# A two-block fp32 network on one core: reciprocal roots of the memory norm and of two head norms on GpSimd, and a new order of work at the ends of the MLPs and of the last head

## The chip, the cores and the metric

One Trainium2 chip, of which the program uses one core. The metric is the device time of one execution in microseconds; the time before is the median of three runs. Engines are named as the profile does: PE is TensorE, DVE is VectorE, ACT is ScalarE, POOL is GpSimd, SP is SyncE, which issues most loads.

## The reference

All in fp32, 512 tokens of width 1024, 256 memory rows, 4 delta-rule heads of 128. Cut to what matters here:

```python
def rmsnorm(x, g):
    return x * rsqrt(mean(x * x, -1) + EPS) * g

def first_block(x, mem, ...):
    h = rmsnorm(x, norm_mix)
    x = x + hybrid_mixer(h, ...)          # chunk gating and a gated delta rule, 4 heads
    m = rmsnorm(mem, norm_mem)            # the memory's norm
    x = x + memory_cross_attention(rmsnorm(x, norm_xa), m, ...)   # keys m @ w_k, values m @ w_v
    x = x + square(relu(rmsnorm(x, norm_ffn) @ w1)) @ w2          # first MLP, width 4096
    return rmsnorm(x, norm_final)

# in hybrid_mixer, for each head:
    o = rmsnorm(gated_delta_rule(q, k, v, g, beta), dn_onorm) * silu(gate)   # the head's output norm
    ... concatenate([y_a, o]) @ w_out

def second_block(x, p, ...):              # mLSTM, sliding-window attention, merge, then
    x = x + square(relu(rmsnorm(x, norm_mlp) @ w_up)) @ w_down    # second MLP
    gate = sigmoid(rmsnorm(x, norm_ple) @ w_ple_gate)
    x = x + gate * (p @ w_ple_proj)       # p is 512 x 256
    return rmsnorm(x, final_norm)
```

## The kernel before

Activations stay in SBUF with features on the partitions, 128 to a tile and 512 tokens wide. A product in fp32 is made of three matmuls on rounded parts (`mm3`, L282 to L284): high by high, high by low and low by high. So every weight granule (`wload`) is loaded by SP into a raw buffer `wr`, rounded by ACT into `wh` (L263) and subtracted by DVE into `wl` (L264); an activation is split in the same way by `split_sb`, ACT L324 or L327 for the high part, DVE L325 or L328 for the remainder. Products of the projections go into three psum banks `psd`; small products of the heads go into banks `c`, two of each kind.

Each engine runs its instructions in the order in which the scheduler put them when the program was built. The scheduler takes what is ready by priority, which is the order of the code unless `high_priority(n)` moves a piece n steps ahead; `issue_after(x)` puts an instruction behind x, and `hold(n)` puts a piece behind the n-th `mm3` that follows.

Norms. `tok_rs` sums the squares `acc` over the partitions with a matmul by ones (L345), DVE adds epsilon (L347), and `rsqrt` takes the reciprocal root: with `power` one POOL instruction (L181), without it eleven small DVE instructions (L186, L187, and three rounds of L189 to L191). `tok_bc` copies the result out wide (DVE L354), transposes it on PE (L357) and copies the psum (ACT L359); that is the scale `bc` with which the psum of the next projection is taken out.

The delta rule. Its four heads run in generators interleaved with the projections. A head inverts a triangular matrix on DVE in 15 steps of two small instructions (L681, L683), with small DMA transfers on SP ahead and behind (L678, L685) and small matmuls after (L661). At its end it takes the norm of its output (L757 to L768: factor `dsc`, scaled output `do`), and `fin` transposes the output (PE L773) and splits it (L327, L328) into `yb`. While heads 2 and 3 run, the memory's norm and its key and value projections (`memory`) are done; keys leave psum by DVE L812. Then `w_out1` multiplies the four heads' `yb` by `w_out_b`, four granules of two output tiles, and adds the result to `x`.

The MLPs. The second product runs by a Strassen-Winograd form, `st_gemm`: per granule, seven products of 12 matmuls of 256 columns into psum banks X, Z (`x` in the rows) and Y (`psd`), each followed by an addition into `x_fm` on DVE (L982) before its bank is used again. `st_weights` loads and splits the parts (L324, L325; the sum of two parts is L959). POOL issues DMA transfers that accumulate sums of weight blocks in memory for it (L229, `sums_ffn_w`), each after copies that ACT's queue issues (L225) have landed. In the last quarter, `post` does the next norm's work for each finished tile: split (L327, L328) and squares (ACT L337, DVE L338). `between` does this for the first MLP, with two sums of squares, and `tail` for the second; `tail` then multiplies `p`, which it splits with L324 and L325, by `w_ple_proj`.

## Time and profile before

| | |
|---|---|
| median of 3 runs | 1700.75 us (1698.43 to 1703.73) |
| the profiled execution | 1699.93 us, of which the span is 1698.1 us |
| PE busy | 1677.7 us, 99% |
| PE weight loads | 1455.5 us, 86% (beside the matmuls) |
| DVE busy | 1207.7 us, 71% |
| ACT busy | 821.5 us, 48% |
| POOL busy | 72.2 us, 4% |
| granted TensorE clock | 1.000 over the span |

The span is what the profiler saw of the program; 1.8 us of the execution lie around it. Busy shares are means over stages. An idle time of PE stands in its timeline in square brackets, with what ended it.

### The profile page before, as it was taken

How to read it: one execution, taken by the hardware profiler on the slowest of the kernel's cores; microseconds unless marked ns; L12 is line 12 of the kernel's file. 1: busy time of each engine (PE TensorE's matmuls, PEld its weight loads, DVE VectorE, ACT ScalarE, POOL GpSimd, SP SyncE). 2: the span in 40 equal slices, each digit the busy share in tenths (PEclk: the TensorE clock that was granted, in tenths of full speed). 3: DMA queues.
4: the chain of work that ended last, by engine and by line, in shares of the span. 5: the costliest groups of instructions: out<-in, count | busy, mean ns of one | idle time of the engine just before them, and what ended most of it. 6: DMA issues, size and time to landing. Idle time of an engine off the chain costs nothing.

```text
span 1698.1 us, 25916 instructions
## 1 busy us (share of the span) xinstructions
PE 1677.7 (99%) x9916; PEld 1455.5 (86%) x9916; DVE 1207.7 (71%) x2521; ACT 821.5 (48%) x1462; POOL 72.2 (4%) x92
## 2 busy tenths in 40 slices
PE   9999999999999999999999999999999999999998
PEld 8988898887898989889988887788888989898987
DVE  6988886656686868688845569865566767676865
ACT  5355755444444444454444457654234444444554
POOL 0200001000000000000000000000000000000000
PEclk9999999999999999999999999999999999999999
DMA  6321366545546464423333332334464464644331
GB/s 203 101 76 52 96 154 180 135 99 174 121 130 170 127 170 128 132 92 110 103 90 97 100 88 69 94 88 115 118 189 126 130 172 124 172 125 133 100 112 50
DMA packets 81947, 205.63 MB, mean 121 GB/s; under 512 B 13088, under 2 KB 14240, under 8 KB 81824
## 3 DMA queue, kind: packets, MB, share of 16 engines
q1 hardware_dynamic: 62672, 169.29, 31.9%
q0 software_dynamic: 9216, 16.78, 7.1%
q10 hardware_dynamic: 9936, 17.91, 3.8%
q8 instruction: 78, 1.28, 0.3%
q14 instruction: 45, 0.37, 0.1%
HBM read 201.59 MB, written 35.65 MB: 140 GB/s over the span
## 4 chain that ended last, share of the span: by engine, by line
PE 88%; DVE 7%; ACT 2%; issue 1%; DMA 1%; SPq 0%; ACTq 0%; DVEq 0%
PE psd L283 21%; PE psd L284 21%; PE psd L282 21%; PE x L282 5%; PE x L283 5%; PE x L284 5%; DVE wl L264 1%; PE c L661 1%; PE c L607 1%; PE lg L1344 1%; PE po L1371 1%; ACT wh L263 1%; DVE S L437 1%; PE m L1265 1%; DVE acc L338 1%
## 5 line engine op out<-in xcount | busy, mean ns | idle before, releaser
L284 PE MATMUL psd<-S,wl 128*128 128x512 f32 (+1 forms) x1256 | 484.1, 386 | 2.6 <-DVE wl L264 2.5
L282 PE MATMUL psd<-S,wh 128*128 128x512 f32 (+1 forms) x1256 | 483.1, 385 | 0.7 <-ACT S L327 0.7
L283 PE MATMUL psd<-S,wh 128*128 128x512 f32 (+1 forms) x1192 | 458.6, 385 | 1.1 <-DVE S L328 0.8
L284 PEld LDWEIGHTS psd<-S,wl 128*128 128x128 f32 x1256 | 236.3, 188 | 48.1 <-DVE wl L264 3.7
L282 PEld LDWEIGHTS psd<-S,wh 128*128 128x128 f32 x1256 | 236.5, 188 | 45.6 <-ACT S L327 1.1
L264 DVE TENSOR_TENSOR wl<-wr,wh 128x1024 fp32r<-128x1024 f32 (+2 forms) x160 | 192.2, 1201 | 116.3 <-ACT wh L263 115.6
L283 PEld LDWEIGHTS psd<-S,wh 128*128 128x128 f32 x1192 | 224.2, 188 | 44.3 <-DVE S L325 1.5
L263 ACT CAST wh<-wr 128x1024 fp32r<-128x1024 f32 (+2 forms) x160 | 163.9, 1026 | 154.7 <-PE psd L283 107.2
L284 PE MATMUL psd<-wh,S 128*128 128x256 f32 (+2 forms) x480 | 135.8, 283 | 0.0
L282 PE MATMUL psd<-wh,S 128*128 128x256 f32 (+2 forms) x480 | 135.7, 283 | 0.0
L283 PE MATMUL psd<-wl,S 128*128 128x256 f32 (+2 forms) x480 | 135.2, 282 | 0.0
L282 PE MATMUL x<-S,wh 128*128 128x256 f32 x452 | 128.0, 285 | 2.9 <-DVE x_fm L982 2.8
L283 PE MATMUL x<-S,wh 128*128 128x256 f32 x452 | 126.5, 281 | 0.0
L284 PE MATMUL x<-S,wl 128*128 128x256 f32 x452 | 126.0, 280 | 0.0
L283 PE MATMUL psd<-S,whx 128*128 128x512 f32 (+1 forms) x296 | 107.8, 364 | 1.0 <-DVE S L325 0.9
L282 PE MATMUL psd<-S,whx 128*128 128x512 f32 (+1 forms) x296 | 107.8, 365 | 0.0
L284 PE MATMUL psd<-S,wlx 128*128 128x512 f32 (+1 forms) x296 | 107.5, 363 | 0.0
L982 DVE TENSOR_TENSOR x_fm<-x_fm,x 128x256 f32<-128x256 f32 x192 | 78.5, 415 | 27.4 <-PE x L284 27.1
L282 PEld LDWEIGHTS psd<-wh,S 128*128 128x128 f32 x480 | 90.4, 189 | 0.3
L283 PEld LDWEIGHTS psd<-wl,S 128*128 128x128 f32 x480 | 90.3, 188 | 0.3
L284 PEld LDWEIGHTS psd<-wh,S 128*128 128x128 f32 x480 | 90.4, 188 | 0.1
L282 PEld LDWEIGHTS x<-S,wh 128*128 128x128 f32 x452 | 84.8, 188 | 5.8 <-DVE x_fm L982 3.1
(455 smaller groups left out, 3176.3 us busy)
## 6 DMA issues: line engine op xcount, KB each, us to landing
wrx<-in_ffn_w_dram SPq DMA_DIRECT2D x32, 512.0 KB
wrx<-in_w_up_dram SPq DMA_DIRECT2D x20, 512.0 KB
wr<-in_w_in_qk_dram SPq DMA_DIRECT2D x16, 512.0 KB
sums_ffn_w<-in_ffn_w_dram ACTq DMA_DIRECT2D x32, 256.0 KB
wr<-in_ffn_w_dram SPq DMA_DIRECT2D x16, 512.0 KB
sums_w_down<-in_w_down_dram ACTq DMA_DIRECT2D x32, 256.0 KB
wr<-in_w_in_v_dram SPq DMA_DIRECT2D x12, 512.0 KB
wr<-in_w_up_dram SPq DMA_DIRECT2D x12, 512.0 KB
```

What stands on the lines that cost most here:

```text
L263: self.last_cast = nc.scalar.copy(hi[:, c], raw[:, c])
L264: nc.vector.tensor_tensor(out=lo[:, c], in0=raw[:, c], in1=hi[:, c].bitcast(F32), op=ALU.subtract)
L282: mm(ps, ah, bh, start=first, stop=False, skip_group_check=more)
L283: mm(ps, ah, bl, start=False, stop=False, skip_group_check=more)
L284: self.last_mm = mm(ps, al, bh, start=False, stop=last, skip_group_check=more)
L338: nc.vector.tensor_tensor(out=acc, in0=acc, in1=sq, op=ALU.add)
L437: nc.vector.tensor_scalar(out=d, in0=d, scalar1=ag[:, j, 0:1], scalar2=r[:, j:j + 1], op0=ALU.subtract, op1=ALU.mult)
L607: nc.tensor.matmul(blk(ps, b), lhs(b), rhs(b), start=True, stop=True)
L661: nc.tensor.matmul(ps[:, b * n:(b + 1) * n], lhs[:, b], rhs(b), start=True, stop=True)
L982: TT(out=x[n][t], in0=x[n][t], in1=ps, op=op)
L1265: nc.tensor.matmul(pX[:, :W], PT[:, tt], va[:, tt], start=True, stop=True)
L1344: nc.tensor.matmul(ps[:, i, K0:], qs[:, 2 * e2 + i, cs], kd[:, w, kc], start=(w == 0), stop=(w == 1))
```

## The change

Six edits, in the order of the program.

1. The output norms of heads 0 and 1 and the norm of the memory take their reciprocal root by the power on POOL in place of the eleven DVE instructions. The memory's `tok_bc` is held behind the 15th `mm3`.
2. In `w_out1` the first granule is written out: k = 0, 1, 2 of both output tiles, then k = 3 (head 3) of both. The cast of the second granule is put behind the cast of head 3's `yb`.
3. In `st_weights` and `st_gemm` the splits, the sum L959 and the additions L982 get a priority 400 steps ahead.
4. The split of a norm's input in `between` and in `tail` gets 200 steps ahead; the squares stay where they were.
5. In `between` the column sums are held behind the 8th `mm3`, and the transposes of the two scales behind the 21st in place of the 16th.
6. In `tail` the split of `p` and the copies of its product get 400 steps ahead.

```diff
 def wload(self, src, kt, n, pieces=None, behind=None):
...
+            with self.tc.issue_after(behind.ins) if behind else nullcontext():
+                self.last_cast = nc.scalar.copy(hi[:, c], raw[:, c])
...
-    def norm_tile(self, k, xh, xl, acc, gname):
-        self.split_sb(xh[k], xl[k], self.x[:, k], self.vcol(gname, k))
+    def norm_tile(self, k, xh, xl, acc, gname, ahead=0):
+        with self.tc.high_priority(ahead):
+            self.split_sb(xh[k], xl[k], self.x[:, k], self.vcol(gname, k))
         self.sq_acc(acc, self.x[:, k], k)
...
-        f = self.rsqrt(mp, so, 4, "do")
+        f = self.rsqrt(mp, so, 4, "do", h < 2)
...
-        for g in range(4):
-            self.proj_fm(self.wgran("w_out_b", g, nk=4), *self.yb, (2 * g, 2 * g + 1), ev)
+        wh, wl = self.wgran("w_out_b", 0, nk=4)
+        (yh, yl), ps = self.yb, [self.psd() for _ in range(2)]
+        for ks in ((0, 1, 2), (3,)):
+            for j in range(2):
+                for k in ks:
+                    c = slice(j * P, (j + 1) * P)
+                    self.mm3(ps[j], wh[k][:, c], wl[k][:, c], yh[k], yl[k], k == 0, k == 3)
+        for j in range(2):
+            ev(j, ps[j])
+        for g in range(1, 4):
+            w = self.wgran("w_out_b", g, nk=4, behind=self.yb_cast if g == 1 else None)
+            self.proj_fm(w, *self.yb, (2 * g, 2 * g + 1), ev)
...
-        rs = self.tok_rs(acc, "rsm", 2)
-        bc = self.tok_bc(rs, "bcm", 2)
+        rs = self.tok_rs(acc, "rsm", 2, power=True)
+        with self.hold(15):
+            bc = self.tok_bc(rs, "bcm", 2)
...
         def split(raw, hi, lo, c=slice(0, 2)):
-            self.split_sb(hi[:, c], lo[:, c], raw[:, c])
+            with self.tc.high_priority(400):
+                self.split_sb(hi[:, c], lo[:, c], raw[:, c])
...
-        nc.vector.tensor_tensor(out=A[0], in0=A[0], in1=B[0], op=ALU.add)
+        with self.tc.high_priority(400):
+            nc.vector.tensor_tensor(out=A[0], in0=A[0], in1=B[0], op=ALU.add)
...
         def add(n, t, ps, op=ALU.add):
-            TT(out=x[n][t], in0=x[n][t], in1=ps, op=op)
+            with self.tc.high_priority(400):
+                TT(out=x[n][t], in0=x[n][t], in1=ps, op=op)
...
-            self.split_sb(xh[o], xl[o], self.x[:, o], g12[:, o:o + 1])
+            with self.tc.high_priority(200):
+                self.split_sb(xh[o], xl[o], self.x[:, o], g12[:, o:o + 1])
...
-            r1 = self.tok_rs(acc, "rs", power=True)
-            ps = self.pss()
+            with self.hold(8):
+                r1 = self.tok_rs(acc, "rs", power=True)
+                ps = self.pss()
...
-            with self.hold(16):
+            with self.hold(21):
...
-            self.norm_tile(o, *ops, "norm_ple_g_2")
+            self.norm_tile(o, *ops, "norm_ple_g_2", 200)
...
-                self.split_sb(ph[:, i], ph[:, 2 + i], raw[:, i])
+                with self.tc.high_priority(400):
+                    self.split_sb(ph[:, i], ph[:, 2 + i], raw[:, i])
```

The rows below are the instructions of one engine in the order in which it runs them. Rows of the changed kernel carry its own line numbers, a few higher than those of before (L265 is L264 of before, L349 is L347, L356 is L354, L329 is L328, L340 is L338, L1000 is L982).

The first place is the memory's norm. On POOL, before, after the last of the products of the first gating stage, the accumulating transfers follow one another:

```order
L442 TENSOR_TENSOR S_42_358<-S_42_358,S_41_357 128x256
L229 DMA sums_ffn_w_0_63<-in_ffn_w_dram 128x512
L229 DMA sums_ffn_w_0_63<-sums_ffn_w_0_63 128x512
L229 DMA sums_ffn_w_1_64<-in_ffn_w_dram 128x512
L229 DMA sums_ffn_w_1_64<-sums_ffn_w_1_64 128x512
```

The same piece after, with `doy` the factor of a head's norm and `rsmy` that of the memory's:

```order
L445 TENSOR_TENSOR S_42_358<-S_42_358,S_41_357 128x256
L181 TENSOR_TENSOR doy_1500<-dso_1489,mhalf 128x4
L229 DMA sums_ffn_w_0_63<-in_ffn_w_dram 128x512
L181 TENSOR_TENSOR doy_1859<-dso_1848,mhalf 128x4
L229 DMA sums_ffn_w_0_63<-sums_ffn_w_0_63 128x512
L181 TENSOR_TENSOR rsmy_2700<-rsmv_2698,mhalf 128x2
L229 DMA sums_ffn_w_1_64<-in_ffn_w_dram 128x512
```

Each of the three powers stands ahead of one of the first three accumulating transfers, and behind the one before it.

On DVE, before, this is a piece of the memory norm's Newton steps (`rsm`), among head 2's inversion; `wl_2756` is the second half of the first key granule:

```order
L189 TENSOR_TENSOR rsmt_2726<-rsmy_2725 128x2
L264 TENSOR_TENSOR wl_2756<-wr_2754,wh_2755 128x1024
L683 TENSOR_TENSOR dV_2283<-dV_2283,dA_402_2284 32x2x14
L190 SCALAR_TENSOR_TENSOR rsmt_2726<-rsmt_2726,rsmv_2722 128x2
L665 TENSOR_TENSOR dT_2825<-dM_2576,masks 128x512
L681 TENSOR_TENSOR dA_402_2284<-dV_2283 32x15
L191 SCALAR_TENSOR_TENSOR rsmy_2725<-rsmt_2726,rsmy_2725 128x2
L675 MEMSET dV_2835 32x256
L683 TENSOR_TENSOR dV_2283<-dV_2283,dA_402_2284 32x15
L189 TENSOR_TENSOR rsmt_2726<-rsmy_2725 128x2
L676 MEMSET dV_2835 32x16
L665 TENSOR_TENSOR dA_402_2284<-dM_2255,masks 128x512
```

And after, from the subtraction for the second key granule's first half over L349 (the sum that the power takes) to the copy L356 (the power's result):

```order
L684 TENSOR_TENSOR dA_398_2260<-dV_2259 32x7x9
L190 SCALAR_TENSOR_TENSOR drt_2503<-drt_2503,dss_2481 128x8
L265 TENSOR_TENSOR wl_2990<-wr_2988,wh_2989 128x1024
L686 TENSOR_TENSOR dV_2259<-dV_2259,dA_398_2260 32x7x9
L191 SCALAR_TENSOR_TENSOR dry_2502<-drt_2503,dry_2502 128x8
L349 TENSOR_SCALAR rsmv_2698<-pss_2695 128x2
L684 TENSOR_TENSOR dA_398_2260<-dV_2259 32x6x10
L189 TENSOR_TENSOR drt_2503<-dry_2502 128x8
L356 COPY e_494_2702<-rsmy_2700 128x256
L686 TENSOR_TENSOR dV_2259<-dV_2259,dA_398_2260 32x6x10
L190 SCALAR_TENSOR_TENSOR drt_2503<-drt_2503,dss_2481 128x8
```

Before, L354 followed six rows further on, fifty behind L347; now the copy stands three rows behind the sum, in the middle of head 2's inversion, and the subtraction for the first key granule's second half has moved far ahead of both.

The second place is the end of the last head, on ACT. Before, `do` is head 3's output, `c_619` its transpose, and `wh_3582` the second granule of `w_out_b`:

```order
L327 ACTIVATE S_592_3237<-psd_3471,rsmy_2725 128x256
L768 ACTIVATE do_2949<-do_2949,dsc_2998 128x128 x4
L263 CAST wh_3582<-wr_3581 128x1024
L327 ACTIVATE S_176_1231<-c_619_3450,vec 128x512
L327 ACTIVATE S_592_3237<-psd_3498,rsmy_2725 128x256
L225 DMA sums_ffn_w_5_68<-in_ffn_w_dram 128x512
L263 CAST wh_3628<-wr_3627 128x1024
```

After, where `c_613` is head 3's transpose and `wh_3546` the second granule:

```order
L328 ACTIVATE S_586_3201<-psd_3435,rsmy_2700 128x256
L328 ACTIVATE S_586_3201<-psd_3462,rsmy_2700 128x256
L771 ACTIVATE do_2913<-do_2913,dsc_2962 128x128 x4
L328 ACTIVATE S_176_1231<-c_613_3414,vec 128x512
L264 CAST wh_3546<-wr_3545 128x1024
L225 DMA sums_ffn_w_5_68<-in_ffn_w_dram 128x512
L264 CAST wh_3592<-wr_3591 128x1024
```

The cast of the second granule went from ahead of the transposed output's rounding to behind it.

The third place is the end of the first MLP, on DVE. Before, in the last quarter:

```order
L328 SCALAR_TENSOR_TENSOR S_1202_7591<-x_fm,g_804_4657,S_1200_7589 128x512
L338 TENSOR_TENSOR acc_7593<-acc_7593,sq_7728 128x512
L338 TENSOR_TENSOR acc_1205_7594<-acc_1205_7594,sq_7731 128x512
L328 SCALAR_TENSOR_TENSOR S_1202_7591<-x_fm,g_804_4657,S_1200_7589 128x512
L325 TENSOR_TENSOR wl_7764<-wr_7742,wh_7763 128x1024
L338 TENSOR_TENSOR acc_7593<-acc_7593,sq_7736 128x512
L338 TENSOR_TENSOR acc_1205_7594<-acc_1205_7594,sq_7739 128x512
L982 TENSOR_TENSOR x_fm<-x_fm,x_7767 128x256
L982 TENSOR_TENSOR x_fm<-x_fm,x_7768 128x256
L982 TENSOR_TENSOR x_fm<-x_fm,psd_7769 128x256
L325 TENSOR_TENSOR wlx_7880<-wrx_7878,whx_7879 128x1024
L982 TENSOR_TENSOR x_fm<-x_fm,x_7767 128x256
```

After, in the same quarter:

```order
L1000 TENSOR_TENSOR x_fm<-x_fm,x_7731 128x256
L329 SCALAR_TENSOR_TENSOR S_1196_7555<-x_fm,g_798_4621,S_1194_7553 128x512
L1000 TENSOR_TENSOR x_fm<-x_fm,x_7732 128x256
L340 TENSOR_TENSOR acc_7557<-acc_7557,sq_7565 128x512
L326 TENSOR_TENSOR wl_7864<-wrx_7842,wh_7863 128x1024
L1000 TENSOR_TENSOR x_fm<-x_fm,x_7731 128x256
L329 SCALAR_TENSOR_TENSOR S_1197_7556<-x_fm,g_798_4621,S_1195_7554 128x512
L1000 TENSOR_TENSOR x_fm<-x_fm,x_7868 128x256
L329 SCALAR_TENSOR_TENSOR S_1197_7556<-x_fm,g_798_4621,S_1195_7554 128x512
L1000 TENSOR_TENSOR x_fm<-x_fm,psd_7870 128x256
L340 TENSOR_TENSOR acc_1199_7558<-acc_1199_7558,sq_7568 128x512
L340 TENSOR_TENSOR acc_7557<-acc_7557,sq_7692 128x512
```

The additions L982 (L1000) stand between single other instructions, and the squares L338 (L340) come late: the square of the first tile stands here ahead of additions of a later granule.

## Rows read from the trace of the kernel before

**Rows 1.** The page: busy time by engine, and the chain that ended last.

```profile
PE 1677.7 (99%) x9916; PEld 1455.5 (86%) x9916; DVE 1207.7 (71%) x2521; ACT 821.5 (48%) x1462; POOL 72.2 (4%) x92
...
PE 88%; DVE 7%; ACT 2%; issue 1%; DMA 1%; SPq 0%; ACTq 0%; DVEq 0%
```

**Rows 2.** Waits of PE: us in total, times, longest.

```profile
PE x L282 <- DVE x_fm L982: 2.8, 3, 1.7
PE psd L284 <- DVE wl L264: 2.5, 3, 1.2
...
PE c L773 <- ACT do L768: 0.2, 1, 0.2
```

**Rows 3.** Timeline of PE, key projection: start, us, line, tiles, [idle before].

```profile
217.40 0.36 PE L283 MATMUL psd<-S,wh 128*128 128x256 f32 x1
218.93 0.39 PE L284 MATMUL psd<-S,wl 128*128 128x256 f32 x1 [1.16 <-DVE wl L264]
...
224.28 0.28 PE L282 MATMUL psd<-S,wh 128*128 128x256 f32 x1
224.40 0.28 PE L283 MATMUL psd<-S,wh 128*128 128x256 f32 x1
225.56 0.39 PE L284 MATMUL psd<-S,wl 128*128 128x256 f32 x1 [0.89 <-DVE wl L264]
```

**Rows 4.** Timeline of DVE in the same stretch.

```profile
212.65 0.16 DVE L347 TENSOR_SCALAR rsmv<-pss 128x2 f32<-128x2 f32 x1 [0.22 <-PE pss L345]
...
217.59 0.14 DVE L189 TENSOR_TENSOR rsmt<-rsmy 128x2 f32<-128x2 f32 x1
217.66 1.21 DVE L264 TENSOR_TENSOR wl<-wr,wh 128x1024 fp32r<-128x1024 f32 x1
...
223.43 0.29 DVE L354 COPY e<-rsmy 128x256 f32<-128x256 f32 x1
```

**Rows 5.** Timeline of PE, first granule of `w_out_b`.

```profile
289.56 0.40 PE L283 MATMUL psd<-S,wh 128*128 128x512 f32 x1
289.80 0.39 PE L284 MATMUL psd<-S,wl 128*128 128x512 f32 x1
290.88 0.50 PE L282 MATMUL psd<-S,wh 128*128 128x512 f32 x1 [0.70 <-ACT S L327]
292.22 0.50 PE L283 MATMUL psd<-S,wh 128*128 128x512 f32 x1 [0.83 <-DVE S L328]
```

**Rows 6.** Timeline of ACT in the same stretch.

```profile
289.20 1.05 ACT L263 CAST wh<-wr 128x1024 fp32r<-128x1024 f32 x1 [2.07 <-DMA wr<-in_w_out_b_dram]
...
290.15 0.68 ACT L327 ACTIVATE S<-c,vec 128x512 fp32r<-128x512 f32 x1
```

**Rows 7.** Timeline of PE, ends of the two MLPs.

```profile
756.95 0.28 PE L283 MATMUL psd<-S,whx 128*128 128x256 f32 x1
758.91 0.38 PE L282 MATMUL x<-S,wh 128*128 128x256 f32 x1 [1.69 <-DVE x_fm L982]
...
1623.41 0.36 PE L282 MATMUL x<-S,wh 128*128 128x256 f32 x1 [0.86 <-DVE x_fm L982]
...
1631.83 0.50 PE L283 MATMUL psd<-S,whx 128*128 128x512 f32 x1 [0.95 <-DVE S L325]
```

**Rows 8.** Timeline of DVE, end of the first MLP.

```profile
757.24 1.28 DVE L338 TENSOR_TENSOR acc<-acc,sq 128x512 f32<-128x512 f32 x2
758.45 0.74 DVE L982 TENSOR_TENSOR x_fm<-x_fm,x 128x256 f32<-128x256 f32 x2
```

**Rows 9.** POOL's powers L181: ns least/median/most; who waited: us, times.

```profile
L181 POOL TENSOR_TENSOR rsy<-rsv,mhalf x2: 1601/1744/1887, 782.0 to 1636.0; 128x4 f32<-128x4 f32 x2
...
L181 POOL TENSOR_TENSOR rs1y<-rs1v,mhalf x1: 695/695/695, 1690.8 to 1690.8; 128x2 f32<-128x2 f32 x1
...
  DVE e L354: 0.9, 1
```

**Rows 10.** Timeline of POOL: its second accumulating transfer.

```profile
212.68 0.82 POOL L229 DMA_DIRECT2D sums_ffn_w<-sums_ffn_w  x1 [28.49 <-DMA sums_ffn_w<-in_ffn_w_dram]
```

More of the change, by code (lines that the diff above doesn't have):

```diff
@@ L252, in wtiles, with wload @@
                 lambda: self.t(p, [P, kt, n], "wl" + x, F32R, bufs=b))
-    def wload(self, src, kt, n, pieces=None):
+    def wload(self, src, kt, n, pieces=None, behind=None):
         nc = self.nc
@@ L262, in wload, with wgran @@
                 then()
-            self.last_cast = nc.scalar.copy(hi[:, c], raw[:, c])
+            with self.tc.issue_after(behind.ins) if behind else nullcontext():
+                self.last_cast = nc.scalar.copy(hi[:, c], raw[:, c])
             nc.vector.tensor_tensor(out=lo[:, c], in0=raw[:, c], in1=hi[:, c].bitcast(F32), op=ALU.subtract)
         return hi, lo
-    def wgran(self, name, g, n=256, nk=8, pieces=None):
+    def wgran(self, name, g, n=256, nk=8, pieces=None, behind=None):
         if self.wx is None:
@@ L273, in wgran @@
         for h in range(nk // 4):
-            parts.append(self.wload(src[g, h], 4, n, pieces if h == 0 else None))
+            parts.append(self.wload(src[g, h], 4, n, pieces if h == 0 else None, behind))
         hi = [parts[k // 4][0][:, k % 4] for k in range(nk)]
@@ L323, in split_sb @@
         if scale is None:
-            nc.scalar.copy(hi, src)
+            cast = nc.scalar.copy(hi, src)
             nc.vector.tensor_tensor(out=lo, in0=src, in1=hi.bitcast(F32), op=ALU.subtract)
         else:
-            nc.scalar.activation(hi, src, AF.Copy, scale=scale)
+            cast = nc.scalar.activation(hi, src, AF.Copy, scale=scale)
             nc.vector.scalar_tensor_tensor(out=lo, in0=src, scalar=scale, in1=hi.bitcast(F32), op0=ALU.mult, op1=ALU.subtract)
+        return cast
     def sq_acc(self, acc, src, k, scale=None, n=T):
@@ L773, in fin @@
                 nc.tensor.transpose(blk(psy, b), o[:, b], ident)
-            self.split_sb(yb_h[:, h], yb_l[:, h], psy, self.vec[:, C_ONORM:C_ONORM + 1])
+            self.yb_cast = self.split_sb(yb_h[:, h], yb_l[:, h], psy, self.vec[:, C_ONORM:C_ONORM + 1])
         yield fin
@@ L1044, in fin @@
             xh, xl, acc, acc2 = ops
-            r1 = self.tok_rs(acc, "rs", power=True)
-            ps = self.pss()
-            for b in range(NB):
-                nc.tensor.matmul(ps[:, b:b + 1], acc2[:, b * P:(b + 1) * P], self.ones[:, 0:1], start=True, stop=True)
+            with self.hold(8):
+                r1 = self.tok_rs(acc, "rs", power=True)
+                ps = self.pss()
+                for b in range(NB):
+                    nc.tensor.matmul(ps[:, b:b + 1], acc2[:, b * P:(b + 1) * P], self.ones[:, 0:1], start=True, stop=True)
             v = self.t(self.tp, [P, NB], "rs2v")
@@ L1397, in ple @@
             for i in range(2):
-                self.split_sb(ph[:, i], ph[:, 2 + i], raw[:, i])
+                with self.tc.high_priority(400):
+                    self.split_sb(ph[:, i], ph[:, 2 + i], raw[:, i])
             pp = [self.slot(i, [P, 4, T]) for i in (2, 3)]
             def ev_p(o, ps):
-                nc.scalar.copy(pp[o // 4][:, o % 4], ps)
+                with self.tc.high_priority(400):
+                    nc.scalar.copy(pp[o // 4][:, o % 4], ps)
             for g in range(4):
```

## The prediction

> **What bounds the kernel.** I read the page first. TensorE is busy for 1677.7 us of a span of 1698.1 us and holds 88% of the chain that ended last [rows 1]. No stage has another limit for long, so an edit is worth only what it takes out of TensorE's idle 20.4 us; time saved on VectorE (71% busy) counts only where TensorE stands waiting for it. The second view is TensorE's waits [rows 2]: the longest lists are a psum bank of the second MLP product that waits for its addition on VectorE, 2.8 us in three waits, and a weight remainder `wl`, 2.5 us in three. The third is TensorE's timeline around those waits [rows 3, 5, 7], and the fourth what VectorE and ScalarE did in the same microseconds [rows 4, 6, 8].
>
> Four places come out of it.
>
> Memory keys: TensorE waits 1.16 us at 218.93 and 0.89 us at 225.56 for `wl` [rows 3]. VectorE started the first of these subtractions at 217.66 only; the norm's Newton steps stand among the inversion of head 2 around it, from L347 at 212.65 to the copy L354 at 223.43 [rows 4].
>
> End of the last head: 0.70 us for the rounded output of head 3 and 0.83 us for its remainder [rows 5]. ScalarE had the cast of the next weight granule in front: it waited 2.07 us for that granule's transfer, ran from 289.20, and the output's L327 started at 290.15 [rows 6].
>
> End of the first MLP: 1.69 us at 758.91 [rows 7]. VectorE did the awaited addition only at 758.45, behind norm work that could wait, at last two additions of squares that started at 757.24 [rows 8].
>
> End of the second MLP: 0.86 us at 1623.41 for the same reason, and 0.95 us at 1631.83 for the remainder of the gate input `p` [rows 7].
>
> With 0.25 us for the third wait for an addition (what [rows 2] has beyond 1.69 and 0.86) and 0.2 us at the transposes L773 [rows 2], the gaps sum to 7.5 us. A gap understates its cost: from 217.40 to 218.93 is 1.53 us where the pitch is 0.12 (224.28 to 224.40), so 1.41 us were lost for a gap of 1.16 [rows 3]; 756.95 to 758.91 loses 1.84 for 1.69 [rows 7]. With 0.15 to 0.25 us on each of nine gaps, about 9 us are lost. That is 0.5% of the time and the most that the edits can remove there.
>
> **The power on GpSimd.** Three Newton chains of eleven instructions leave VectorE and three powers come to GpSimd. Such an instruction takes 0.14 us, and the next starts 0.07 us later where it doesn't depend on it [rows 4]: 33 x 0.07 to 0.14 is 2.3 to 4.6 us of VectorE. In the memory norm L354 stood 10.8 us behind L347; now it stands three rows behind it and VectorE waits there for the power. The only such copy in the trace waited 0.9 us [rows 9], so I take 0.9 us. Behind it in VectorE's queue are the rest of head 2's inversion, head 3's decay masks L636 and the second half of the second key granule's `wl`. The power itself took 0.70 us alone and 1.60 and 1.89 us in the two cases where a 1.2 us VectorE subtraction of two SBUF tensors ran beside it [rows 9]. The powers of the two heads have such work beside them (`wl` for head 0, a 0.4 us addition of squares for head 1); that work is their cover, and without it VectorE would stand for 0.9 us each time.
>
> The Trainium skill (SBUF — State Buffer, section "SBUF: two separate sides") says that VectorE with two SBUF inputs and a GpSimd operation that reads SBUF take one port pair in turn, each holding it for its whole instruction. The slow powers agree with it. By the rule head 1's power starts only behind the addition beside it, and VectorE waits for it too, 0.4 + 0.7 us less the addition itself: the sum below would be -5.5 instead of -6.2.
>
> The `wl` of the first two key granules stand earlier and the column sums L345 later, among the first key matmuls. Removed: 1.16 + 0.89 us of gaps, 2.4 us from start to start. Given back: head 2's inversion, L643 and the second half of the second granule's `wl` now follow the 0.9 us wait, and the bank that L643 frees is wanted a few matmuls later. Bounds: 0 (the wait is absorbed) and 2.1 us (wait plus one 1.2 us subtraction in front of L643). I take 1.0, nearer the row of the wait. Net **-1.4**.
>
> On SyncE, loads of the key weights move ahead of head 2's small transfers L685; a load waits for the `wl` that frees its buffer, but that `wl` stands ahead of the inversion's last step, which L685 needs anyway: 0.
>
> **End of the last head.** The cast of granule 1 now waits for head 3's rounding, and granule 0 does k = 0 to 2 of both halves before head 3's k = 3: 18 matmuls at 0.23 us (289.56 to 289.80 [rows 5]) cover 4.1 us instead of 9 with 2.1. The work to hide is four transposes, L327 and L328, about 1.0 + 0.7 + 0.7 us, so 0.70 + 0.83 + 0.2 go. The postponed cast hides behind granule 0's 24 matmuls, 5.6 us; were its transfer as late as now (the cast ends at 290.25 [rows 6], its remainder 1.2 us later), about 1 us is left. Bounds: 0 and 2.2; I take **-2.1**.
>
> **Ends of the MLPs.** Additions L982, weight splits and L959 go first, norm roundings second, squares L338 last. A product gives VectorE 12 x 0.12 = 1.4 us until its bank is wanted again; between two additions stands now at most one 1.2 us operation, or an L328 with a square. I leave 0.2 us of waits at each end and take -2.0 of 2.1 and 0.9 of 1.0: **-2.9**. The squares that are put off end some 5 us after the last addition, and the column sums are held eight groups of matmuls back; the next product has three banks, 24 x 0.23 = 5.5 us each, before it wants the scale. If that cover were gone, TensorE would stand for the rest of the norm's chain, 1 to 5 us. The split of `p` goes ahead of the last norm roundings: the 0.95 gap goes, **-1.0**.
>
> **Sum.** -1.4 - 2.1 - 2.9 - 1.0 = -7.4. Some hundred rows of TensorE change places between 200 and 290 us and in each quarter of the MLPs, where now nothing waits. I charge 1.2 us, five waits as small as the 0.2 and 0.25 above; bounds 0 and 4. So -6.2: from the profiled execution's 1699.93 to 1693.7. The median of the runs is 0.8 us above that execution, hence **1694.5**.
>
> **Rivals.** *All nine gaps go and nothing comes back*: -8 to -10, 1691 to 1693. For it: every awaited instruction stands earlier. Against: the 0.9 us wait for GpSimd is certain. *The gains are half given back*: the key projection keeps a wait (bank of L643, or `wl` still late) and the reordered head steps cost 2 to 4 us: 1697 to 1701. For it: TensorE has 1% of slack [rows 1], so nearly every row moved in front of an awaited one shows as a new wait, and the 0.9 us wait lies in the queue that the key projection's banks hang on. Against: what is moved back is mostly squares, which nothing awaits soon. *Slower*: the memory norm's power stands behind GpSimd's second accumulating transfer, which waited 28.49 us for a landing until 212.68 [rows 10]. L347 comes near 216 (some 30 key and small matmuls later than at 212.65). If that landing slips beyond about 216, L354 slips with it and all of VectorE's queue behind it; once the three banks of the key projection are full, some 6 us later, each further us is a us of TensorE. To be 6 us slower after the 7.4 gained, the landing must come near 236. For it: nothing but the order of the queue. Against: no transfer is added in front of it. 1703 to 1707, little chance.
>
> **Numbers.** Runs of this kernel spread by some 5 us, and 0.3% (5.1 us) is about what tells a change from none. All gone 0.18, forecast (1692.8 to 1695.6) 0.39, half given back 0.36, slower 0.07. Faster by over 0.3%, below 1695.65, is the first two, 0.57; within 0.3% is the third, 0.36. The range leaves out the slower case and about half a tenth at either end: from 1690.5 (9 us gone plus 1 from the relief of VectorE) to 1700.
>
> **What the profile after would show.** Right: no wait for `wl` L264 over 0.5 us near 219 and 225; POOL's L181 between the first accumulating transfers, VectorE idle 0.7 to 1.2 us ahead of L354; L327 of head 3 ahead of the cast and TensorE without a gap at `w_out_b`'s k = 3; no wait for L982 over 0.3 us; TensorE idle near 13 us. Wrong: a new wait at L601, L607 or L661 between 200 and 260 us, L354 released by a power that started long after L347, or a wait for `bc` in the products that follow an MLP.

## The result, and the profile after

The changed kernel takes 1706.43 us (median of 20 runs, 1700.80 to 1710.49) against 1699.52 us (20 runs, 1698.26 to 1703.73) of the kernel before on the same chips; the ratio is 1.0038, interval 1.0030 to 1.0046. It is slower by 0.38%, where 1694.5 us, a gain, was forecast.

The profiled execution took 1709.38 us, of which the span is 1707.6 us. From its page, in the order busy time, granted clock over 40 slices, chain that ended last, against [rows 1]:

```profile
PE 1687.8 (99%) x9916; PEld 1464.7 (86%) x9916; DVE 1209.5 (71%) x2488; ACT 822.5 (48%) x1462; POOL 75.9 (4%) x95
...
PEclk9999998999999999999999999999999999999999
...
PE 90%; DVE 6%; ACT 2%; issue 1%; DMA 1%; POOL 0%; SPq 0%; ACTq 0%; DVEq 0%; POOLq 0%
```

Subtract busy time from the span first. TensorE is idle for 1707.6 - 1687.8 = 19.8 us, where it was 20.4. The forecast had 13. So there are as many gaps as before, though not the same ones. And the same 9916 matmuls are busy 10.1 us longer, while the clock, 1.000 in every slice before, has one slice (the seventh, 256 to 299 us) below 0.9. The span's 9.5 us are 10.1 of slower matmuls less 0.6 of idle time. Two separate things went wrong.

**The gaps.** TensorE's waits, against [rows 2] (us in total, times, longest):

```profile
PE c L664 <- DVE dTb L690: 3.4, 2, 2.6
PE pss L347 <- DVE acc L340: 2.5, 1, 2.5
...
PE psd L285 <- DVE wl L265: 0.5, 1, 0.5
...
PE c L776 <- ACT do L771: 0.3, 1, 0.3
```

The list has no row for `x_fm` any more, none for the roundings at `w_out_b` and none for the split of `p`, and of the three waits for `wl` only the one of 0.5 us is left, near 70 us, at which no edit aimed. The nine gaps on which the forecast rests are gone but for the 0.2 to 0.3 us at the transposes. In their place stand three waits that the kernel before had not: 0.87 us at 178 us, 2.52 at 218 and 2.57 at 267. Before's 20.4 - 7.5 for the gaps aimed at, + 0.87 + 2.52 + 2.57, is 18.9; measured 19.8.

**The wait at 218** is for the last square of a memory tile, ahead of the column sums L347. First SP's queue of before in a timeline, with the last two of the eight memory tiles ahead of the next key load (two had gone out from 177.87 on):

```profile
202.09 1.18 SPq L802 DMA_DIRECT2D e<-in_mem_dram  x2
205.95 0.33 SPq L260 DMA_DIRECT2D wr<-in_xa_wk_dram  x1
```

Then the same stretch after, the rows of five engines in order of time; the eighth memory tile now stands behind a key load:

```profile
207.04 1.15 POOL L181 TENSOR_TENSOR doy<-dso,mhalf 128x4 f32<-128x4 f32 x1 [21.73 <-DVE dA L684]
208.23 0.16 DVE L768 TENSOR_TENSOR dsc<-dsc,doy 128x4 f32<-128x4 f32 x1 [0.94 <-POOL doy L181]
208.40 1.21 DVE L265 TENSOR_TENSOR wl<-wr,wh 128x1024 fp32r<-128x1024 f32 x1
209.63 0.33 SPq L260 DMA_DIRECT2D wr<-in_xa_wk_dram  x1
...
210.87 0.47 DVE L329 SCALAR_TENSOR_TENSOR S<-e,vec,S 128x256 fp32r<-128x256 f32 x1
211.12 0.88 POOL L229 DMA_DIRECT2D sums_ffn_w<-sums_ffn_w  x1 [2.92 <-DMA sums_ffn_w<-in_ffn_w_dram]
...
211.41 0.33 SPq L816 DMA_DIRECT2D e<-in_mem_dram  x1
...
215.33 0.28 PE L284 MATMUL psd<-S,wh 128*128 128x256 f32 x1
215.45 0.28 PE L285 MATMUL psd<-S,wl 128*128 128x256 f32 x1
216.64 0.51 ACT L328 ACTIVATE S<-e,vec 128x256 fp32r<-128x256 f32 x1 [2.84 <-DMA e<-in_mem_dram]
...
217.79 0.40 DVE L340 TENSOR_TENSOR acc<-acc,sq 128x256 f32<-128x256 f32 x1
218.25 1.01 PE L347 MATMUL pss<-ones,acc 128*128 128x1 f32 x4 [2.52 <-DVE acc L340]
219.13 0.56 PE L283 MATMUL psd<-S,wh 128*128 128x256 f32 x1
219.49 0.41 PE L284 MATMUL psd<-S,wh 128*128 128x256 f32 x1
219.70 0.41 PE L285 MATMUL psd<-S,wl 128*128 128x256 f32 x1
...
220.00 0.71 POOL L181 TENSOR_TENSOR rsmy<-rsmv,mhalf 128x2 f32<-128x2 f32 x1 [8.00 <-DVE rsmv L349]
220.74 0.29 DVE L356 COPY e<-rsmy 128x256 f32<-128x256 f32 x1 [0.63 <-POOL rsmy L181]
```

Read it backwards. TensorE needs `acc`; its last addition L340 starts at 217.79, because the tile's split came at 216.64, because ACT waited 2.84 us for the tile's transfer. That was issued at 211.41, where before the last two memory tiles were issued from 202.09 on, and it landed 5.2 us later.

The issue was late for two reasons. A key load of 512 KB stands ahead of it in SP's queue; it went out at 209.63, just when the subtraction `wl` that began at 208.40 ended (+ 1.21). What came last, though, was the tile's buffer: the split L329 of an earlier tile freed it at 211.34. Subtraction and split both stand on DVE behind L768, which waited 0.94 us for head 1's power, and DVE had no pause between L768 and that split.

The landing was late because of what ran beside it, or so it seems: GpSimd's accumulating transfer of 256 KB was issued at 211.12. In the DMA view SP's queue moved 0.16 MB between 212.6 and 216.3 us (this tile and the end of the key load) and GpSimd's 0.26 MB; between 205.4 and 207.4, with GpSimd's queue at rest, SP's moved 0.26 MB, the two memory tiles before this one. So the key load was nearly through when the tile's data began to move. In all kernels here with this wait for `acc` the last memory tile was issued within half a microsecond of that transfer, and in all others over 7 us ahead of it. No run takes the transfer away and leaves the loads, so its share of the 5.2 us isn't shown.

**The wait at 267** is at head 3's inversion, for the small transfers `dY`:

```profile
266.61 0.29 DVE L690 TENSOR_TENSOR dTb<-dY,masks 128x128 f32<-128x128 f32 x1 [2.46 <-DMA dY<-dV]
266.95 1.08 PE L664 MATMUL c<-dTb,dT 128*128 128x32 f32 x8 [2.57 <-DVE dTb L690]
```

The inversion's last step on DVE ended at 259.31, 7.3 us ahead of L690; in the kernel before it was 5.0 us (249.92 to 254.96). Here too GpSimd's queue was at work beside the small transfers: 0.25 MB between 262 and 266.6, before 0.07 MB between 251 and 254. That this made them slow isn't shown either.

**The clock.** The last rows of PE above stand 0.21 us apart where before the wait they stood 0.12 apart (215.33 to 215.45). Windows of 5 us around both waits (the clock is the third figure from the right: the granted clock, then DMA share and GB/s):

```profile
210.00:215.00 5.00, 4.79 (x35) 4.20 (x34) 4.80 (x25) 3.80 (x15) 0.88 (x1) 1.00 0.70 163
215.00:220.00 5.00, 2.48 (x15) 2.27 (x14) 2.81 (x12) 1.75 (x3) 0.00 (x1) 0.79 0.12 23
220.00:225.00 5.00, 5.00 (x26) 5.00 (x26) 3.22 (x24) 1.22 (x3) 0.71 (x1) 0.53 0.35 105
225.00:230.00 5.00, 5.00 (x46) 5.00 (x45) 4.38 (x9) 3.36 (x10) 0.00 (x0) 1.00 0.50 130
...
265.00:270.00 5.00, 3.05 (x22) 3.05 (x23) 2.77 (x8) 1.06 (x4) 0.81 (x1) 0.91 0.71 158
270.00:275.00 5.00, 5.00 (x26) 5.00 (x25) 1.50 (x4) 1.00 (x4) 0.00 (x0) 0.50 0.52 122
275.00:280.00 5.00, 5.00 (x26) 5.00 (x25) 1.60 (x3) 1.91 (x4) 0.00 (x0) 0.50 0.25 70
280.00:285.00 5.00, 5.00 (x35) 4.45 (x34) 2.40 (x3) 2.90 (x6) 0.81 (x1) 0.73 0.47 121
```

Behind each wait the clock went from its upper level (2.4 GHz) to the lower (1.2 GHz) and TensorE, busy all the time, worked 26 matmuls off in 5 us instead of 46. What the full clock lacks, (0.21 + 0.47) x 5 + (0.09 + 0.50 + 0.50 + 0.27) x 5, is 10.2 us: all of the growth of TensorE's busy time.

The Trainium skill (TensorE: Matmul & The Clock Gate, section "Part 1: The HAM clock gate (the "warmup" mystery)") says that the array's clock is at half rate by default and that activity releases it; the rows agree on the half rate, with 0.21 us for a matmul of 256 columns against 0.12.

### The profile page after: what moved, and what is told of

Its sections match the earlier page's. It is cut to its first block, busy times and chain, and to the rows that moved or that the text cites. A ratio compares the mean times of both kernels' runs of the same rounds, so it can differ in the third digit from the quotient of the medians.

```text
span 1707.6 us, 25861 instructions
## 1 busy us (share of the span) xinstructions
PE 1687.8 (99%) x9916; PEld 1464.7 (86%) x9916; DVE 1209.5 (71%) x2488; ACT 822.5 (48%) x1462; POOL 75.9 (4%) x95
## 4 chain that ended last, share of the span: by engine, by line
PE 90%; DVE 6%; ACT 2%; issue 1%; DMA 1%; POOL 0%; SPq 0%; ACTq 0%; DVEq 0%; POOLq 0%
PE psd L284 21%; PE psd L285 21%; PE psd L283 21%; PE x L283 6%; PE x L284 5%; PE x L285 5%; DVE wl L265 1%; PE c L664 1%; PE c L610 1%; PE lg L1364 1%; PE po L1391 1%; DVE S L440 1%; PE m L1285 1%; ACT wh L264 1%; PE c L283 0%
## 5 line engine op out<-in xcount | busy, mean ns | idle before, releaser
L265 DVE TENSOR_TENSOR wl<-wr,wh 128x1024 fp32r<-128x1024 f32 (+2 forms) x160 | 192.1, 1201 | 113.2 <-ACT wh L264 112.7
L264 ACT CAST wh<-wr 128x1024 fp32r<-128x1024 f32 (+2 forms) x160 | 163.9, 1026 | 153.9 <-PE psd L284 109.2
L1000 DVE TENSOR_TENSOR x_fm<-x_fm,x 128x256 f32<-128x256 f32 x192 | 79.5, 417 | 24.4 <-PE x L285 22.9
L283 PE MATMUL x<-S,whx 128*128 128x256 f32 x316 | 90.7, 287 | 0.0
```

The source lines that it names most:

```text
L264: self.last_cast = nc.scalar.copy(hi[:, c], raw[:, c])
L265: nc.vector.tensor_tensor(out=lo[:, c], in0=raw[:, c], in1=hi[:, c].bitcast(F32), op=ALU.subtract)
L283: mm(ps, ah, bh, start=first, stop=False, skip_group_check=more)
L1000: TT(out=x[n][t], in0=x[n][t], in1=ps, op=op)
```

## The experiments

The kernel before ran in the same rounds each time, with medians of 1699.67 to 1700.05 us; differences in us are to those medians or, where it is said, to another kernel here.

**The power taken out, and put in alone.** The first kernel undoes edit 1, the second makes edit 1 alone.

```diff
-        f = self.rsqrt(mp, so, 4, "do", h < 2)
+        f = self.rsqrt(mp, so, 4, "do")
...
-        rs = self.tok_rs(acc, "rsm", 2, power=True)
-        with self.hold(15):
-            bc = self.tok_bc(rs, "bcm", 2)
+        rs = self.tok_rs(acc, "rsm", 2)
+        bc = self.tok_bc(rs, "bcm", 2)
```

> The changed kernel with the first edit undone: Newton steps on VectorE for all norms of that region, no hold; the edits of w_out_b, the MLP ends and the tail stay. Theory A (the first edit alone makes the loss, through the order that the scheduler finds with it: two new TensorE waits of 2.5 us at L347 and L664, and a granted clock near one half behind each): both waits and the clock loss are gone, and the key projection's two waits of before (1.16 and 0.89) are back; the other gains of some 6 us stay: 1692 to 1695, clock 1.000. Rival B (the new waits come from the reordered w_out_b or from the priorities): 1704 to 1710, the waits still there.

> The kernel before with the first edit alone (three powers on GpSimd and the hold of the memory's transposes). Theory A: the order of loads around the memory tiles is that of the changed kernel, so the waits of 2.5 us at L347 and L664 and the clock loss are all there, and the waits at the ends of the last head and of the MLPs stay too: 1706 to 1714, in the profile a clock of 0.993 to 0.999. Rival B: 1697 to 1701, clock 1.000.

Without the power 1695.29 us (1693.96 to 1696.08, 5 runs), ratio 0.9969 (0.9957 to 0.9981); the power alone 1713.08 us (1706.71 to 1716.57, 6 runs), ratio 1.0070 (1.0051 to 1.0089). So edits 2 to 6 gain 4.4 us by the medians, 5.3 by the ratio, and edit 1 costs 11 to 13 us, with them or without. The waits of the second show the same two places, and one more:

```profile
PE c L661 <- DVE dTb L687: 3.8, 2, 2.9
...
PE pss L345 <- DVE acc L338: 2.5, 1, 2.5
PE c L773 <- ACT do L768: 1.9, 1, 1.9
```

while without the power the old row is back and none of these:

```profile
PE psd L285 <- DVE wl L265: 2.5, 3, 1.2
```

**Edits 2 and 3 to 6, each group alone on the kernel before** (the diffs are those of the change):

> The kernel before with the second edit alone (granule 0 of w_out_b in the order k = 0 to 2, then 3; the next cast behind head 3's rounding). By the prediction's term, -2.1 us: 1697 to 1698.3, TensorE without the waits of 0.70 and 0.83 us there. Rival: the waits move to the next granule's cast and nothing is won: 1699 to 1700.

> The kernel before with the third to sixth edits alone (priorities at the ends of the MLPs and in the tail). By the prediction's terms, -2.9 - 1.0 us: 1695 to 1697, without the waits of 1.69, 0.86 and 0.95 us. Rival: the order of the quarters gives part of it back: 1697 to 1700.

Edit 2 alone: 1697.62 us (1695.94 to 1705.46, 12 runs), ratio 0.9988 (0.9977 to 0.9998), 2.2 us less than the 1699.82 of before. Edits 3 to 6 alone: 1695.61 us (1694.30 to 1699.38, 7 runs), ratio 0.9972 (0.9959 to 0.9985), 4.2 us less. By the medians both groups do what their rows promised, 6.4 us in sum; together, in the kernel without the power, they gain 4.4 to 5.3.

The profiled execution of edit 2 alone was the longest of its twelve, 1705.46 us at a mean clock of 0.995. TensorE's waits in the key projection are those of the kernel before, 1.16 us at 219 and 0.89 at 225.5; yet the clock was 0.71, 0.50, 0.50 and 0.92 in the four stretches of 5 us from 225 to 245. The kernel before has such an execution too: one of its 25 in those rounds took 1706.25 us at 0.995.

**The two parts of the power apart.** Edits 2 to 6 with the power for heads 0 and 1 only; with the power and the hold for the memory only; and the latter without the hold.

```diff
-        rs = self.tok_rs(acc, "rsm", 2, power=True)
-        with self.hold(15):
-            bc = self.tok_bc(rs, "bcm", 2)
+        rs = self.tok_rs(acc, "rsm", 2)
+        bc = self.tok_bc(rs, "bcm", 2)
```

> The changed kernel with the power for the norms of heads 0 and 1 alone; the memory's norm keeps its Newton steps and is not held. The order of SyncE's queue is that of the changed kernel up to the last memory tile (a load of key weights ahead of it). Theory A1 (the late load of the last memory tile is what counts, and the heads' powers bring it): the wait at L347 for the sum of squares is there, 1.5 to 3 us, and the clock falls behind it: 1698 to 1708. Rival A2 (the waits of VectorE for the powers, 0.9 us each, are what counts, whichever norm has them): two of three waits, some 1696 to 1699, no wait over 1 us at L347.

```diff
-        f = self.rsqrt(mp, so, 4, "do", h < 2)
+        f = self.rsqrt(mp, so, 4, "do")
```

> The changed kernel with the power for the memory's norm alone, and its hold; the heads keep their Newton steps. The memory tiles are loaded in the order of before. Theory A1: no wait at L347 over 0.5 us and no fall of the clock there; the wait for head 3's inversion at L664 may stay: 1691 to 1697. Rival A2: one of three waits, 1694 to 1697. Rival A3 (the memory's power and the hold make the loss): 1703 to 1710.

```diff
-        f = self.rsqrt(mp, so, 4, "do", h < 2)
+        f = self.rsqrt(mp, so, 4, "do")
...
-        with self.hold(15):
-            bc = self.tok_bc(rs, "bcm", 2)
+        bc = self.tok_bc(rs, "bcm", 2)
```

> The power for the memory's norm alone, without the hold; the rest of the change as it is. The hold is what differs from the run before it that had power and hold for the memory alone (1698.5 us). If the hold and the order that comes with it made that run's waits for a cast and for the inversion (1.3 us each), this one comes to 1693 to 1695.5; if the power's own wait moves the head's chain, 1697 to 1699.

Heads only: 1708.38 us (1705.45 to 1711.28, 6 runs), ratio 1.0050; the whole loss. It has the wait for `acc` (2.46 us at 217), but in its profile the clock fell only behind two later waits (the last section has the rows). Memory only: 1698.48 us (1696.48 to 1704.28, 12 runs), ratio 0.9991 (0.9982 to 1.0001), 3 us above the kernel without a power and outside all three ranges that I gave it (1.5 us above the nearest), with no wait for `acc`. Without the hold: 1708.51 us (1703.55 to 1713.68, 7 runs), ratio 1.0043; I had expected the hold to matter little and was wrong, it is worth 10 us here. Its waits are two for `dTb` (1.23 and 1.78 us) and one of 1.36 for a cast, and the clock is down from 225 to 250 and from 265 to 270. So 13 us can be lost without a wait for `acc` and with the memory's loads in the order of before.

**The memory tiles first.** The changed kernel with the loads, splits and squares of the memory 300 steps ahead:

```diff
+            with self.tc.high_priority(300):
-            raw = self.t(self.tp, [P, M], "e1")
+                raw = self.t(self.tp, [P, M], "e1")
...
```

> The changed kernel, all three powers kept, with the loads, splits and squares of the memory tiles given a priority 300 steps ahead: two more memory tiles are loaded ahead of the third load of key weights, and the sum of squares stands some 25 rows earlier on VectorE. Theory A1 (the wait at L347 comes from the late last memory tile): that wait is gone or under 1 us and the clock does not fall behind it; head 3's inversion, whose row hardly moves, may still be awaited at L664: 1697 to 1704. Rival A2 (VectorE's waits for GpSimd and the port are the loss): no change beyond 1 us against the changed kernel at the same clock: 1703 to 1709.

1700.13 us (1696.62 to 1705.74, 12 runs), ratio 1.0002 (0.9989 to 1.0014): 6.3 us less than the changed kernel, all three powers still in it. The wait for `acc` is gone; of the new waits 0.86 and 1.13 us for `dTb` are left. The 6.3 us are not the price of the wait for `acc` alone: the edit also brought the wait at head 3's inversion from 2.57 to 1.13 us, and the changed kernel measured again (below) is 4.5 us above this one.

**The wait filled.** Twelve matmuls without use (each is two in the trace's counts) ahead of the L664 that waited at 267:

```diff
+            if fill:
+                self.fill(fill, ps[:, 256:384], lhs[:, 0], lhs[:, 1], after)
...
+            psY = mmp(Mx, lambda b: T_[:, b], 32, 12 if h == 3 and lv == 16 else 0, cut)
```

> The changed kernel, with twelve extra 128x128 fp32 matmuls on TensorE right ahead of head 3's first L664 (the product of dT by dTb, which waited 2.57 us at 266.95); they write columns of its psum bank that nothing reads, and the real work waits for dTb as long as before. The loads on SP and the instructions of POOL keep their order. Theory A (the loss is mainly the granted clock that falls behind the wait: 1 - 0.91, 0.50, 0.50 and 0.73 over four stretches of 5 us is 6.8 us in the profiled run): clock 1.00 from 265 to 285, median 1700.5 to 1703. Theory B (the loss is the waits themselves and what they push back): the same products start at the same time, 1705.5 to 1707.5, whatever the clock shows.

> The changed kernel again, as it is, on the same chip and in the same rounds as the one with the filled wait. Both theories: 1705 to 1708, with runs from 1701 at a clock of 0.999 to 1710 at 0.993.

The filled kernel took 1707.39 us (1706.37 to 1712.46, 5 runs), the changed one beside it 1704.66 us (1700.79 to 1710.10, 12 runs). By its number this is theory B's, but the profile shows why it tells less than it was made for:

```profile
264.68 2.84 PE L295 MATMUL c<-dT 128*128 128x128 f32 x24
267.73 1.08 PE L676 MATMUL c<-dTb,dT 128*128 128x32 f32 x8 [0.22 <-DVE dTb L702]
268.65 0.37 PE L284 MATMUL psd<-wl,S 128*128 128x256 f32 x1
270.79 1.08 PE L676 MATMUL c<-dY,dV 128*128 128x32 f32 x8 [1.42 <-ACT dY L713]
```

```profile
265.00:270.00 5.00, 4.15 (x35) 3.75 (x33) 2.49 (x7) 0.69 (x3) 0.81 (x1) 1.00 0.83 180
270.00:275.00 5.00, 4.21 (x30) 4.18 (x31) 1.78 (x4) 1.47 (x6) 0.00 (x0) 0.85 0.47 126
275.00:280.00 5.00, 5.00 (x25) 4.61 (x25) 1.02 (x2) 2.18 (x5) 0.00 (x0) 0.50 0.02 5
280.00:285.00 5.00, 5.00 (x47) 4.60 (x47) 2.82 (x5) 2.43 (x4) 0.81 (x1) 0.97 0.51 157
```

The filler kept the clock at 1.00 through the stretch in which it stands, but the edit also changed TensorE's order: between this L664 and the next of the same chain stand 4 matmuls of the product beside it, where the changed kernel has 16 (267.87 to 270.23). TensorE came to the next step early, waited 1.42 us there, and the clock fell behind that. So a wait of 2.57 us was not needed for a fall, and the two theories are not told apart.

**The other way to an early `wl`.** Edits 2 to 6 without a power, the first two key granules 30 steps ahead:

```diff
-            self.proj_fm(self.wgran("xa_wk", g), ah, al, (2 * g, 2 * g + 1), ev_k, ncol=M)
+            with self.tc.high_priority(30 if g < 2 else 0):
+                wk = self.wgran("xa_wk", g)
+            self.proj_fm(wk, ah, al, (2 * g, 2 * g + 1), ev_k, ncol=M)
```

> Without any power (edits 2 to 6 alone, 1695.3 measured), and the loads, casts and subtractions of the first two key granules 30 steps ahead, which is the other way to take the subtraction wl out of the memory norm's way. Theory A (the fall of the clock follows a wait of some 2.5 us, and small waits only cost themselves): the waits of 1.15 and 0.87 us at 216.78 and 223.80 go and 1693 to 1694.5 remains. Theory B (whatever moves the key weights ahead delays the memory's last squares, here from row 449 to 479 of VectorE, and gives a wait for acc at L347 as in the changed kernel): 1697 to 1703, clock below 0.998.

1702.29 us (1695.42 to 1704.50, 12 runs), ratio 1.0004 (0.9993 to 1.0016). The time is theory B's, the place is not: there is no wait for `acc`; TensorE waits 1.55 us at 225 for `wl` and 1.80 us at 228 for `dTb`, and the clock is at 0.50 from 230 to 240. This kernel gives the clearest look at the clock. Its twelve runs are one program with one order: three took 1695.4 to 1696.1 us at a mean clock of 0.999 to 1.000, nine took 1701.7 to 1704.5 at 0.993 to 0.996, and none lies between. The 32 runs of the changed kernel (20 and 12) are nearly alike: 15 at 0.997 to 0.999, 1700.8 to 1705.5 (median 1702.5), 14 at 0.993 or 0.994, 1707.8 to 1710.5 (median 1709.9), three at 0.996 between.

**Each head's power alone**, on edits 2 to 6:

```diff
-        f = self.rsqrt(mp, so, 4, "do")
+        f = self.rsqrt(mp, so, 4, "do", h == 0)
```

> Edits 2 to 6 and the power for head 0 alone (edits 2 to 6 alone: 1695.3 measured; with the power for heads 0 and 1: 1708.4). Theory A (it is the order of SP's loads that costs: with head 0's power the program, as built, has a key load ahead of the memory tiles' loads, and the last memory tile behind the next key load): TensorE waits some 2 us or more for acc at L347, the clock falls in most runs, 1702 to 1710. Theory B (each power costs VectorE's wait of 0.9 us and what hangs on it, wherever the loads stand): head 0 and head 1 share the 13 us about equally, 1700 to 1703 each.

```diff
-        f = self.rsqrt(mp, so, 4, "do")
+        f = self.rsqrt(mp, so, 4, "do", h == 1)
```

> Edits 2 to 6 and the power for head 1 alone. The loads of the memory tiles and of the first key weights keep the order of before in the program as built. Theory A: no wait for acc at L347, 1694 to 1698, clock 0.998 or more in most runs. Theory B: 1700 to 1703.

Head 0's power alone: 1706.20 us (1703.99 to 1708.05, 5 runs), ratio 1.0035 (1.0022 to 1.0048). Head 1's alone: 1698.73 us (1697.03 to 1704.73, 12 runs), ratio 0.9994 (0.9985 to 1.0004). Against the 1695.3 of no power that is 10.9 and 3.4 us: nearer to theory A, with head 1 0.7 us above its range. Two of theory A's signs failed: the wait for `acc` with head 0's power is 1.6 us and not some 2 or more, and with head 1's the clock was at 0.998 in only four of twelve runs, below that in the rest. The waits of the first:

```profile
PE c L664 <- DVE dTb L690: 4.3, 3, 2.4
PE psd L285 <- DVE wl L265: 2.1, 2, 1.6
PE pss L347 <- DVE acc L340: 1.6, 1, 1.6
```

Behind the wait of 1.6 us for `acc` the clock did not fall; it stayed at 1.00 from 215 to 230 and was 0.58, 0.50, 0.50 and 0.71 from 230 to 250, behind 1.57 us for `wl` at 227 and 2.36 for `dTb` at 231. So the 10.9 us are the price of the whole order that comes with head 0's power, not of one late tile.

The second has no wait for `acc`, and 1.37 us for `dTb` at 223 is the longest in this part of the program. In its profiled execution, one of three of its twelve runs with a mean clock of 0.994 (the other nine had 0.997 or 0.998), even that was followed by half clock:

```profile
220.00:225.00 5.00, 3.33 (x23) 3.06 (x22) 4.70 (x12) 1.42 (x4) 0.81 (x1) 0.87 0.46 64
225.00:230.00 5.00, 5.00 (x26) 5.00 (x25) 1.66 (x4) 0.06 (x1) 0.00 (x0) 0.50 0.78 226
230.00:235.00 5.00, 5.00 (x25) 5.00 (x25) 3.33 (x11) 1.21 (x2) 0.00 (x0) 0.50 0.00 0
235.00:240.00 5.00, 5.00 (x24) 5.00 (x25) 1.61 (x8) 2.20 (x5) 0.00 (x0) 0.50 0.55 157
```

The profiled executions side by side (span, TensorE busy, their difference, mean clock):

| kernel | span | busy | idle | clock |
|---|---|---|---|---|
| before | 1698.1 | 1677.7 | 20.4 | 1.000 |
| changed | 1707.6 | 1687.8 | 19.8 | 0.994 |
| edit 1 alone | 1714.8 | 1688.2 | 26.6 | 0.991 |
| edits 2 to 6 | 1692.7 | 1676.1 | 16.6 | 1.000 |
| changed, memory tiles first | 1700.8 | 1685.3 | 15.5 | 0.995 |
| edits 2 to 6, keys first | 1702.5 | 1683.7 | 18.8 | 0.995 |

Idle time differs by up to 11 us between them and busy time by 12; neither tells the span alone. The changed kernel with the memory tiles first has the least idle time of all and is still 8 us longer than edits 2 to 6, by its busy time.

## Why the prediction was wrong

*Ends of the MLPs* (-2.9), *the split of `p`* (-1.0) and *end of the last head* (-2.1) were right one by one: 4.2 measured for the first two terms together against 3.9, 2.2 for the third. All three together gain 4.4 to 5.3, where the terms sum to 6.0; the difference stays open.

*The power on GpSimd* (net -1.4, bounds 0 to 2.1 given back) is where it failed, at the step "On SyncE ...: 0". I looked at the key loads against head 2's transfers L685, and not at the memory tiles' loads in the same queue. In the program as built the last of those tiles is loaded 8.5 us later than before (211.41, before at 202.9), behind a key load and a buffer that both hang on VectorE's work behind a power, and at the same time as a transfer of GpSimd's; its square is the last thing that the column sums need, and TensorE waits 2.52 us. That the place of the memory tiles brings this wait is shown: put first, they end it, with all three powers in; with head 1's power alone, which leaves their order, it doesn't come; with head 0's power alone, which changes it, it does (1.6 us). How much of the loss is due to it is not shown: the kernels in which it is taken away or left out lose 3.2 to 13.2 us against the one without a power all the same.

The step on the cover failed as well. The forecast had VectorE wait once, 0.9 us at the memory's copy, and not at the two heads, whose powers have work beside them. VectorE waited 0.92 us for head 0's power, behind a `wl` of 1.21 us beside it, 0.94 for head 1's and 0.63 for the memory's. The trace of before had shown it: the copy L354 of [rows 9] waited its 0.93 us behind a `wl` that had run beside the power (from 1635.80, 1.23 us).

The Trainium skill's rule on the port that VectorE and GpSimd share (SBUF — State Buffer, section "SBUF: two separate sides"), by which head 1's power would take longer beside the addition of squares, agrees: it took 1.15 us beside them, head 0's 2.04 beside a `wl`, and one of the same 128x4 form 1.00 with VectorE at rest (at 796). The memory's, of 128x2, took 0.71.

*The reorder charge* (1.2 us, bounds 0 and 4) was too small. The three new waits are 0.87 + 2.52 + 2.57 = 6.0 us. Without the one at 218, which is the step above, 3.4 us are left, inside the bounds. They stand at the inversion's L664 (L661 of before), which I named among the places that would show the forecast wrong, though for 200 to 260 us, and they came at 178 and 267.

*What no step had* is the clock. Every price in the forecast is a microsecond of TensorE for a microsecond of its wait, at a clock that was 1.000 throughout the trace. In the profiled execution the two long waits cost 5.1 us as waits and 10.2 more as half clock behind them. In the median of the runs it is less, since the fall doesn't come in each: the runs of the changed kernel at 0.997 and more have a median of 1702.5, those at 0.994 or less 1709.9.

The rival *slower* came true by its sign, and not by its mechanism: GpSimd's second accumulating transfer ran at 211.12, the memory's sum L349 came at 219.77 and its power at once, at 220.00. That transfer of GpSimd's did not hold the power; it ran beside the late tile's load. *All nine gaps gone and nothing back* was right in its first half only. *Half given back*, 1697 to 1701, named the right engines, and was short by the clock.

What stays open: why the scheduler, given head 0's power, puts the memory's loads in another order, was not looked into. Not shown is what the late tile would cost with GpSimd's transfer elsewhere. Nor can it be told which of two waits in a run lowered the clock where they lie close, or how much of the 3 us that remain between the memory's power and none is wait and how much clock. That the falls of the clock come from the waits is argued only: each fall between 170 and 310 us in these traces stands at or behind a wait of TensorE, but the waits of the kernel before were followed by one in edit 2 alone and by none in its own trace, and no run here has the same order without the wait.

The version to keep is edits 2 to 6 without a power: 1695.29 us, faster than both.

## What to carry to other kernels

When an instruction moves to another engine, follow the queue of every engine that its old neighbours feed, down to the loads: here 33 small VectorE instructions less moved one 128 KB load behind one of 512 KB and into the time of a GpSimd transfer. Where TensorE is the bound and its clock is 1.000, price a new wait of a microsecond and more at several times its length, with a chance: in these traces it could be followed by some three to twenty microseconds at half clock. And compare busy time as well as idle time; if the same instructions got longer, look at the clock before looking for a cause among the waits.

## What the runs showed of the hardware

One program, in one order, ran at two speeds some 7 us apart: the edits 2 to 6 with the keys first, with the mean clock at 0.993 to 0.996 or at 0.999 and more. Length alone doesn't tell which waits are followed by half clock: 1.69 us at 757 in the kernel before [rows 7] was not in its trace, 2.46 us at 217 with the power for the heads alone was not either, 1.16 and 0.89 us at 219 and 225.5 were not in the kernel before but were with edit 2 alone, and in the run with the heads' powers 1.62 and 1.12 us, ending within three microseconds of each other, were:

```profile
225.00:230.00 5.00, 3.38 (x29) 3.17 (x28) 3.35 (x8) 0.89 (x2) 0.30 (x1) 1.00 0.52 73
230.00:235.00 5.00, 3.75 (x22) 3.43 (x22) 3.08 (x10) 0.87 (x4) 0.00 (x0) 0.78 0.62 204
235.00:240.00 5.00, 5.00 (x26) 4.63 (x24) 2.54 (x11) 2.55 (x7) 0.00 (x0) 0.50 0.00 0
```

The Trainium skill (TensorE: Matmul & The Clock Gate, section "A second HAM failure mode: psum-queue depth-cycling") tells of a kernel whose clock swings because TensorE idles briefly and often between groups of matmuls. Two short waits ahead of one fall point the same way; a clock that swings again and again is not in this trace.
